# A trunk of float32 feed-forward stages in split products: the order of a pair's matmuls varied from stage to stage

## The chip, the cores and the metric

One core of one Trainium2 chip runs the whole program in one launch. The metric is the device time of that launch in microseconds (us). TensorE (PE) multiplies, and its weight loads stand on a row of their own (PEld); VectorE (DVE) and ScalarE (ACT) do the elementwise work; SyncE (SP) issues the transfers from memory.

## What is computed

Four layers of a decoder trunk on 256 tokens of 1024 features, all in float32. The part that the change touches is the feed-forward stage, of which each layer has two:

```
def swiglu(x, w_gate_up, w_down):              # x [256, 1024], w_gate_up [1024, 2 * 2816], w_down [2816, 1024]
    g, u = jnp.split(x @ w_gate_up, 2, axis=-1)
    return (jax.nn.silu(g) * u) @ w_down

for i in range(4):
    h = h + 0.5 * swiglu(rms_norm(h, norm_ffn1[i]), ffn1_w_gate_up[i], ffn1_w_down[i])
    h = h + mixer[i % 3](rms_norm(h, norm_mix[i]))   # stick-breaking, MoBA or latent attention
    h = h + 0.5 * swiglu(rms_norm(h, norm_ffn2[i]), ffn2_w_gate_up[i], ffn2_w_down[i])
return rms_norm(h, final_norm)
```

## The kernel before

**Split products.** TensorE takes the 4-byte type float32r, which holds fewer bits than float32. So each float32 value is split into a high part and a low part, and a product `w.T @ x` is the sum of high by high, high by low and low by high. The first name is the stationary operand (loaded into the array, 128 x 128), the second the moving one (streamed through, 256 tokens). The moving operand of a feed-forward stage holds a row block's 256 high columns and its 256 low columns side by side. `wide` (L432) therefore makes one product of two matmuls: the high stationary part with 512 moving columns (L434) into a whole bank of PSUM, and the low stationary part with the 256 high columns (L435) into the bank's lower half. `both` (L442, L443) adds the two halves of a bank afterwards. This text calls the first matmul W, the second L, and both together a pair. The mixers use two other forms: `mm3` (L428 to L430) makes three matmuls of 256 columns (stationary parts high, high, low), and `x_proj` (L475 to L477) keeps activations stationary (high, high, low) and streams weights, mostly 512 columns.

**A feed-forward stage.** `ffn` runs `gate_up` for 22 column blocks j of the hidden layer: 8 row blocks k, and for each k one pair for the gate (bank `bs[0]`) and one for the up half (bank `bs[1]`). That is 352 pairs. Two k are issued as one op of the scheduler (one k for the first three j of the program). Then 8 output blocks m each take 22 pairs into one bank, issued in ops of 3, 3, 3 and 2 pairs for each half of the hidden layer: 176 pairs. The stages are numbered here 0 to 7 in the order in which they run, two for each layer with a mixer between them.

**Weights.** A `Chunk` is one transfer into a `raw` buffer (4 of them). ACT copies it into a high part `whi` (L314) and DVE subtracts to get the low part `wlo` (L321), in pieces of up to 1024 columns; there are 6 pairs of such buffers. A piece's buffers come free when the last op that uses it is done.

**Order.** Nothing is ordered by hand. `Program` holds a graph of ops with estimated costs, and `emit` puts them in order by a list schedule: each engine takes the ready op with the lowest due time. One op's instructions stay together. `prep` and `square` (L342 to L345) square each finished row block of h on ACT into one of two `sq` buffers and add it to `acc` on DVE; `norm` then sums over partitions with four short matmuls (L403) and spreads the result with two transposes (L408), which land inside the next stage's products.

Of the kernel before, what the change touches and what calls it, by code (L numbers as in the profile page):

```python
# [28 lines left out]
ZC = SEQ + P  # columns of a head's scores that causality leaves  # L29
# [12 lines left out]
# Gains in one table, 128 rows of a norm to a column.  # L42
# [9 lines left out]
class Slots:  # L52
    """Room for a number of like buffers; some of them are kept from work that can wait."""
# [15 lines left out]
class Buf:  # L69
    """A buffer that the first op of its use takes and the last one gives back."""  # L70
# [7 lines left out]
class Op:  # L78
    """A run of instructions: `ways` has its cost and its emitter for each engine that can do it."""
# [6 lines left out]
class Program:  # L86
    """The program as a graph of short runs of instructions. `emit` puts them in order by a list
    scheduling on estimated costs: each engine's next is the ready one with the least priority
    number, which is the tensor engine's nominal time (us) at the op's place."""
# [32 lines left out]
    def copy(self, cols, fn, deps=(), n=1, **kw):  # L122
        """fn(engine's copy) by whichever of ScalarE and VectorE comes to it first."""
        return self.either({"ACT": (n * 0.095 + 0.00083 * cols, lambda: fn(self.on_act)),
                            "DVE": (n * 0.07 + 0.00104 * cols, lambda: fn(self.on_dve))}, deps, **kw)

    def emit(self):
# [3 lines left out]
        events = []  # time, number, op that becomes ready or buffer that becomes free  # L131
# [58 lines left out]
def fast(n, cols=SEQ):  # L190
    """Time of n float32r products."""
# [4 lines left out]
def trunk_kernel(ctx: ExitStack, tc: tile.TileContext, a: dict, out: bass.AP, nsub: int = 3 * DEPTH):  # L196
# [23 lines left out]
    # ---- room on the chip  # L220
# [5 lines left out]
    parts = Slots([(cp.tile([P, HALF], F32R, name=f"whi{i}"), cp.tile([P, HALF], F32R, name=f"wlo{i}"))  # L226
# [5 lines left out]
    squares = room(2, [SEQ], "sq")  # L232
# [3 lines left out]
    # The normed rows and the activations: a row block's high parts, then its low ones.  # L236
# [8 lines left out]
    # In a mixer the activations' room holds the heads' outputs, then split softplus or latents.  # L245
# [11 lines left out]
    # ---- the tensor engine's clock rises with work: zeros, until the first data come  # L257
# [6 lines left out]
    # ---- constants  # L264
# [8 lines left out]
    # jp[p, i] = i - p  # L273
# [9 lines left out]
    # ---- the weights: DMA, then an exact split of each float32 value into two float32r parts  # L283
    class Chunk:
        """`n` row blocks of `w` columns, `per` of them to a piece. The program's first chunks come
        and are split in smaller runs of row blocks, between `cuts`, the loads in the order `lead`."""

        def __init__(self, ap, n, w, per, cuts=None, lead=20.0):
            self.w, self.per = w, per
# [22 lines left out]
        def hi_fn(self, raw, b, i, k, e):  # L312
            w = self.w
            return lambda: nc.scalar.activation(b.ap[0][:, (k - i) * w:(e - i) * w], raw.ap[:, k * w:e * w], AF.Copy)  # L314

        def lo_fn(self, raw, b, i, k, e):
            w = self.w

            def f():
                s = slice((k - i) * w, (e - i) * w)  # L320
# [3 lines left out]
        def get(self, k):  # L324
            s = slice(k % self.per * self.w, (k % self.per + 1) * self.w)
# [12 lines left out]
    # ---- norms  # L338
    def square(m, dep, lead):
        """Row block m's share of the mean square; gives the op that adds it."""  # L340
# [6 lines left out]
    def prep(m, gain_at, dep, start=False):  # L347
        """Row block m of h is final: its gained, split form for the next products, or its share
        of the result, still to be divided by the rms."""
# [12 lines left out]
    def result(m, dep):  # L362
        """Row block m, gained, transposed into the banks of the result."""
# [14 lines left out]
    def rsqrt(v, scale, keep):  # L378
        """(v * scale + EPS) ** -0.5 of a [128, 2] tile, by Newton's method."""
# [3 lines left out]
        # x is -1/2 of the radicand; the first guess comes from its bits.  # L383
# [657 lines left out]
```

## Time and profile before

| | us |
|---|---|
| median of 3 runs | 1963.67 |
| lowest, highest | 1962.95, 1966.06 |
| span of the profiled execution, first to last instruction | 1960.8 |
| median less that span | 2.9 |

The trace is of one execution. Only its span is recorded, so the 2.9 us around it is the difference from the median. Times in the trace count from the first instruction. A row of the timeline has the start in us, the duration in us, the engine, the line, the operation, the names of the tiles (written<-read), the shapes and a count. The recorded duration of a matmul contains a fixed stretch after its last column, so neighbouring matmuls overlap in the record; the pace is read from start to start.

### The profile page before, as it was taken

Reading aid. Unit: us, or ns where it says so; the run is one execution under the profiler, and the core shown is the slowest. Engines: PE = TensorE matmul, PEld = TensorE weight load, DVE = VectorE, ACT = ScalarE, POOL = GpSimd, SP = SyncE. Lnnn points to the kernel's source line nnn. Section 1 sums busy time; section 2 is a strip of 40 time slices with the busy share of each in tenths; the row PEclk is TensorE's granted clock in tenths of the full one; section 3 lists DMA queues with packets and bytes.
Section 4 is the critical chain, followed back from the end, with each engine's and each line's share of the span. In section 5 each row is a group of like instructions: output and inputs, shape, how many; then the busy total and the mean of one; then the engine's idle time right before and its main releaser. Section 6 shows DMA issues by size and latency. Waiting matters only on the chain.

```text
span 1960.8 us, 30578 instructions
## 1 busy us (share of the span) xinstructions
PE 1946.6 (99%) x11681; PEld 1696.5 (87%) x11681; DVE 1452.3 (74%) x2661; ACT 1144.1 (58%) x2119; POOL 0.4 (0%) x5
## 2 busy tenths in 40 slices
PE   9999999999999999999999999999999999999997
PEld 7888989888888878888888888988888888898886
DVE  8777767777777777877677768877677766668864
ACT  7555556555555555655555557755555555665553
POOL 0000000000000000000000000000000000000000
PEclk9999999999999999999999999999999999999999
DMA  8546435546654653554655454355465456435542
GB/s 301 184 146 220 163 129 175 191 147 204 208 181 147 221 181 109 178 188 147 214 199 191 141 178 155 126 197 178 151 213 197 165 168 220 148 125 198 177 151 81
DMA packets 55875, 342.79 MB, mean 175 GB/s; under 512 B 6192, under 2 KB 7088, under 8 KB 26928
## 3 DMA queue, kind: packets, MB, share of 16 engines
q1 hardware_dynamic: 55728, 340.84, 50.6%
q8 instruction: 92, 1.51, 0.3%
q14 instruction: 55, 0.45, 0.1%
HBM read 339.76 MB, written 1.05 MB: 174 GB/s over the span
## 4 chain that ended last, share of the span: by engine, by line
PE 98%; ACT 1%; DVE 0%; DMA 0%; SPq 0%; issue 0%; DVEq 0%; ACTq 0%
PE ps L434 50%; PE ps L435 26%; PE ps L428 3%; PE ps L429 3%; PE ps L430 3%; PE ps L475 3%; PE ps L476 2%; PE ps L477 2%; PE ps L574 1%; PE ps L624 1%; PE ps L733 1%; PE ps L698 1%; PE ps L771 1%; PE ps L596 1%; PE ps L562 0%; PE ps L576 0%
## 5 line engine op out<-in xcount | busy, mean ns | idle before, releaser
L314 ACT ACTIVATE whi<-raw 128x1024 fp32r<-128x1024 f32 (+2 forms) x738 | 703.0, 954 | 729.7 <-PE ps L434 527.3
L321 DVE TENSOR_TENSOR wlo<-raw,whi 128x1024 fp32r<-128x1024 f32 (+2 forms) x738 | 804.2, 1091 | 396.7 <-ACT whi L314 388.6
L434 PE MATMUL ps<-x,whi 128*128 128x512 f32 x2816 | 998.3, 398 | 1.0 <-DVE acc L345 0.8
L435 PE MATMUL ps<-x,wlo 128*128 128x256 f32 x2816 | 791.8, 281 | 0.2 <-DVE wlo L321 0.2
L434 PEld LDWEIGHTS ps<-x,whi 128*128 128x128 f32 x2816 | 529.7, 188 | 132.2 <-ACT whi L314 2.5
L435 PEld LDWEIGHTS ps<-x,wlo 128*128 128x128 f32 x2816 | 528.8, 188 | 1.3 <-DVE wlo L321 1.2
L434 PE MATMUL ps<-a,whi 128*128 128x512 f32 x1408 | 498.8, 398 | 0.0
L435 PE MATMUL ps<-a,wlo 128*128 128x256 f32 x1408 | 395.7, 281 | 0.0
L434 PEld LDWEIGHTS ps<-a,whi 128*128 128x128 f32 x1408 | 264.8, 188 | 65.1
L435 PEld LDWEIGHTS ps<-a,wlo 128*128 128x128 f32 x1408 | 264.4, 188 | 0.0
L443 DVE TENSOR_TENSOR mid<-ps,mid 128x256 f32<-128x256 f32 x416 | 173.5, 417 | 9.6 <-ACT mid L442 9.6
L442 ACT ACTIVATE mid<-ps 128x256 f32<-128x256 f32 x416 | 151.3, 367 | 11.9 <-PE ps L435 11.9
L515 DVE TENSOR_TENSOR mid<-mid 128x256 f32<-128x256 f32 x176 | 74.6, 424 | 14.2 <-DVE mid L443 0.5
L510 DVE TENSOR_TENSOR mid<-mid,rb 128x256 f32<-128x256 f32 x176 | 74.7, 424 | 6.4 <-ACT rb L411 0.9
L475 PE MATMUL ps<-whi,x 128*128 128x512 f32 (+2 forms) x192 | 74.4, 388 | 0.0
L517 DVE TENSOR_TENSOR a<-mid,a 128x256 fp32r<-128x256 f32 x176 | 73.4, 418 | 1.0 <-ACT a L516 1.0
L428 PE MATMUL ps<-a,whi 128*128 128x256 f32 x256 | 73.9, 289 | 0.0
L428 PE MATMUL ps<-x,whi 128*128 128x256 f32 x256 | 73.0, 285 | 0.0
L476 PE MATMUL ps<-wlo,x 128*128 128x512 f32 (+2 forms) x192 | 72.9, 380 | 0.0
L511 ACT ACTIVATE mid<-mid 128x256 f32<-128x256 f32 x176 | 71.8, 408 | 1.8 <-DVE mid L510 1.7
L477 PE MATMUL ps<-whi,x 128*128 128x512 f32 (+2 forms) x192 | 72.7, 379 | 0.0
L429 PE MATMUL ps<-a,whi 128*128 128x256 f32 x256 | 71.5, 279 | 0.0
(128 smaller groups left out, 1636.7 us busy)
## 6 DMA issues: line engine op xcount, KB each, us to landing
raw<-in_ffn_gu SPq DMA_DIRECT2D x173, 1024.0 KB, 4.8
raw<-in_ffn_dn SPq DMA_DIRECT2D x128, 704.0 KB, 4.1
raw<-in_sb_qk SPq DMA_DIRECT2D x16, 1024.0 KB, 4.9
raw<-in_moba_qkv SPq DMA_DIRECT2D x12, 1024.0 KB, 4.8
raw<-in_sb_v SPq DMA_DIRECT2D x8, 1024.0 KB, 4.7
raw<-in_sb_o SPq DMA_DIRECT2D x8, 1024.0 KB, 4.7
raw<-in_moba_o SPq DMA_DIRECT2D x4, 1024.0 KB, 4.8
raw<-in_mla_o SPq DMA_DIRECT2D x4, 1024.0 KB, 5.0
```

Source lines behind the costliest of these rows:

```text
L314: return lambda: nc.scalar.activation(b.ap[0][:, (k - i) * w:(e - i) * w], raw.ap[:, k * w:e * w], AF.Copy)
L321: nc.vector.tensor_sub(b.ap[1][:, s], raw.ap[:, k * w:e * w], b.ap[0][:, s].bitcast(F32))
L428: nc.tensor.matmul(o, wh, mh, start=first, stop=False, skip_group_check=True)
L429: nc.tensor.matmul(o, wh, ml, start=False, stop=False, skip_group_check=True)
L434: nc.tensor.matmul(o, wh, m2.rearrange("p a b -> p (a b)"), start=first, stop=False, skip_group_check=True)
L435: nc.tensor.matmul(o[:, :SEQ], wl, m2[:, 0, :], start=False, stop=last, skip_group_check=True)
L442: x = g.act(SEQ, lambda: nc.scalar.activation(o(), b.ap[:, SEQ:], AF.Copy), [last], take=take, lead=lead)
L443: return g.dve(SEQ, lambda: nc.vector.tensor_add(o(), b.ap[:, :SEQ], o()), [x], free=[b], lead=lead)
L475: nc.tensor.matmul(o, xs[0][:, k, ts], hi, start=(k == 0), stop=False)
L476: nc.tensor.matmul(o, xs[0][:, k, ts], lo, start=False, stop=False)
L477: nc.tensor.matmul(o, xs[1][:, k, ts], hi, start=False, stop=(k == n - 1))
L510: o = g.dve(SEQ, lambda: nc.vector.tensor_mul(x(), x(), rb[:, 0, :]), [o, rbs[0]])
```

## The change

Every feed-forward stage issues the matmuls of its pairs through a new function `products`, in an order given by two tables, one for gate and up (first and second half of the column blocks j) and one for the down products (first and second half of the output blocks m). The mathematical products are the same in every order. The orders are, for one pair or a group of pairs:

- `each`: W L W L, as before; `each_up`: the same with L added to the bank's upper half; `low_first`: L W L W.
- `three`: the wide matmul is cut in two, high by high into the lower half and high by low into the upper half, each of 256 columns and each with its own load of the same high part, and then L; `three_low_first` has L ahead of them.
- `all`, `all_up`, `all_low_first`, `all_three`: all pairs of the group take the first part, then all the next one (W W L L, for instance). In the gate and up products `pair_all...` groups the two pairs of one k, and plain `all` groups the four pairs of an op; in the down products the group is the op's 3 or 2 pairs.
- `bank`: the op's pairs of one bank together (W W L L), then those of the other.

A number beside an order of gate and up is a shift: the stationary parts are written and read that many float32 elements further on in their buffers. To make room, each `whi` and `wlo` buffer grows by 16 elements, and there is one `sq` buffer in place of two. The estimated costs of the scheduler are the same as before. The diff, without removed comments and texts:

```diff
+ORDERS = [[("each", 0), ("each_up", 0)], [("pair_all", 0), ("pair_all_up", 0)],
+          [("three", 0), ("three_low_first", 0)], [("low_first", 0), ("pair_all_low_first", 0)],
+          [("all", 0), ("bank", 0)], [("each", 16), ("each", 4)],
+          [("pair_all_three", 0), ("three", 16)], [("each", 8), ("each", 0)]]
+DOWN_ORDERS = [["each", "each_up"], ["all", "all_up"], ["three", "three_low_first"], ["low_first", "all_low_first"],
+               ["all_three", "all_three"], ["each", "each"], ["each_up", "all_up"], ["each", "each"]]
...
-    parts = Slots([(cp.tile([P, HALF], F32R, name=f"whi{i}"), cp.tile([P, HALF], F32R, name=f"wlo{i}"))
+    parts = Slots([(cp.tile([P, HALF + 16], F32R, name=f"whi{i}"), cp.tile([P, HALF + 16], F32R, name=f"wlo{i}"))
...
-    squares = room(2, [SEQ], "sq")
+    squares = room(1, [SEQ], "sq")
...
-            w = self.w
-            return lambda: nc.scalar.activation(b.ap[0][:, (k - i) * w:(e - i) * w], raw.ap[:, k * w:e * w], AF.Copy)
+            w, o = self.w, self.shift
+            return lambda: nc.scalar.activation(b.ap[0][:, o + (k - i) * w:o + (e - i) * w], raw.ap[:, k * w:e * w], AF.Copy)
...
-                s = slice((k - i) * w, (e - i) * w)
+                s = slice(self.shift + (k - i) * w, self.shift + (e - i) * w)
...
-            s = slice(k % self.per * self.w, (k % self.per + 1) * self.w)
+            s = slice(self.shift + k % self.per * self.w, self.shift + (k % self.per + 1) * self.w)
...
+    def products(order, items, k0, k1):
+        started, left = set(), {}
+
+        def put(item, part, cols):
+            o, hi, lo, m2, k = item
+            key = id(o)
+            first = k == k0 and key not in started
+            started.add(key)
+            left[key] -= 1
+            last = k == k1 and left[key] == 0
+            w, m, at = ((hi, m2.rearrange("p a b -> p (a b)"), slice(0, 2 * SEQ)),
+                        (lo, m2[:, 0, :], slice(0, SEQ)),
+                        (lo, m2[:, 0, :], slice(SEQ, 2 * SEQ)),
+                        (hi, m2[:, 0, :], slice(0, SEQ)),
+                        (hi, m2[:, 1, :], slice(SEQ, 2 * SEQ)))[part]
+            nc.tensor.matmul(o[:, at], w, m, start=first, stop=last, skip_group_check=True)
+
+        WIDE, LOW, LOW_UP, HH, HL = range(5)
+        kinds = {"each": [WIDE, LOW], "each_up": [WIDE, LOW_UP], "low_first": [LOW, WIDE],
+                 "three": [HH, HL, LOW], "three_low_first": [LOW, HH, HL],
+                 "all": [WIDE, LOW], "all_up": [WIDE, LOW_UP], "all_low_first": [LOW, WIDE],
+                 "all_three": [HH, HL, LOW], "bank": [WIDE, LOW]}
+        parts_ = kinds[order]
+        for it in items:
+            left[id(it[0])] = left.get(id(it[0]), 0) + len(parts_)
+        if order.startswith("all"):
+            for part in parts_:
+                for it in items:
+                    put(it, part, None)
+        elif order == "bank":
+            for key in dict.fromkeys(id(it[0]) for it in items):
+                for part in parts_:
+                    for it in items:
+                        if id(it[0]) == key:
+                            put(it, part, None)
+        else:
+            for it in items:
+                for part in parts_:
+                    put(it, part, None)
...
-                            wide(bs[p].ap, hi[:, w], lo[:, w], x2[:, k], k == 0, k == NT - 1)
+                            items.append((bs[p].ap, hi[:, w], lo[:, w], x2[:, k], k))
+                    if order in ("each", "each_up", "low_first", "three", "three_low_first"):
+                        for i in range(0, len(items), 2):
+                            products(order, items[i:i + 2], 0, NT - 1)
+                    elif order.startswith("pair_"):
+                        for i in range(0, len(items), 2):
+                            products(order[5:], items[i:i + 2], 0, NT - 1)
+                    else:
+                        products(order, items, 0, NT - 1)
...
-            evac(j, *gate_up(j, cuts, lead, 1 if first else 2))
+            order, shift = ORDERS[2 * l + which][j >= NF // 2]
+            evac(j, *gate_up(j, cuts, lead, 1 if first else 2, order, 0 if first else shift))
...
+            order = DOWN_ORDERS[2 * l + which][m >= NT // 2]
...
-                        for f in fs:
-                            j = half * FH + f
-                            wide(b.ap, *c.get(f), a2[:, j], j == 0, j == NF - 1)
+                        items = [(b.ap, *c.get(f), a2[:, half * FH + f], half * FH + f) for f in fs]
+                        if order.startswith("all") or order == "bank":
+                            products(order, items, 0, NF - 1)
+                        else:
+                            for it in items:
+                                products(order, [it], 0, NF - 1)
```

## Rows read from the trace of the kernel before

**Rows 1.** The page: its first line, the busy time of each engine (us, share of the span, instructions), and the chain of work that ended last by engine.

```profile
span 1960.8 us, 30578 instructions
...
PE 1946.6 (99%) x11681; PEld 1696.5 (87%) x11681; DVE 1452.3 (74%) x2661; ACT 1144.1 (58%) x2119; POOL 0.4 (0%) x5
...
PE 98%; ACT 1%; DVE 0%; DMA 0%; SPq 0%; issue 0%; DVEq 0%; ACTq 0%
```

**Rows 2.** The waits, longest first: who waited for whom, us in total, times, longest. First the longest of all engines, then two of the longest of PE.

```profile
ACT whi L314 <- PE ps L434: 527.3, 482, 3.2
...
PE ps L372 <- ACT nat L373: 2.3, 1, 2.3
...
PE ps L434 <- DVE acc L345: 0.8, 1, 0.8
```

**Rows 3.** The down products of stage 0: the count of W matmuls (ns min/median/max, first and last start), and from PE's timeline the first W, the last W and the mixer's first matmul behind its L.

```profile
L434 PE MATMUL ps<-a,whi x176: 397/398/398, 132.6 to 194.4; 128*128 128x512 f32 x176
...
132.57 0.40 PE L434 MATMUL ps<-a,whi 128*128 128x512 f32 x1
...
194.41 0.40 PE L434 MATMUL ps<-a,whi 128*128 128x512 f32 x1
...
194.76 0.28 PE L428 MATMUL ps<-x,whi 128*128 128x256 f32 x1
```

**Rows 4.** PE's groups by line and shape over the whole span: count, busy us, mean ns of one, idle before.

```profile
L434 PE MATMUL ps<-x,whi 128*128 128x512 f32 x2816 | 998.3, 398 | 1.0 <-DVE acc L345 0.8
L435 PE MATMUL ps<-x,wlo 128*128 128x256 f32 x2816 | 791.8, 281 | 0.2 <-DVE wlo L321 0.2
...
L429 PE MATMUL ps<-x,whi 128*128 128x256 f32 x256 | 71.4, 279 | 0.0
...
L476 PE MATMUL ps<-wlo,x 128*128 128x512 f32 x160 | 62.8, 392 | 0.0
```

**Rows 5.** `mm3` in the output projection after the first mixer: the count of its first matmul, and from the timeline the first and the last of them.

```profile
L428 PE MATMUL ps<-a,whi x41: 281/281/282, 295.9 to 310.1; 128*128 128x256 f32 x41
...
295.93 0.28 PE L428 MATMUL ps<-a,whi 128*128 128x256 f32 x1
...
310.07 0.28 PE L428 MATMUL ps<-a,whi 128*128 128x256 f32 x1
```

**Rows 6.** `mm3` in the output projection after the second mixer: the same rows, then the W of two pairs in a row, among the first of stage 3, right behind it.

```profile
L428 PE MATMUL ps<-a,whi x30: 276/276/277, 789.4 to 799.2; 128*128 128x256 f32 x30
...
789.38 0.28 PE L428 MATMUL ps<-a,whi 128*128 128x256 f32 x1
...
799.24 0.28 PE L428 MATMUL ps<-a,whi 128*128 128x256 f32 x1
...
799.92 0.40 PE L434 MATMUL ps<-x,whi 128*128 128x512 f32 x1
...
800.27 0.40 PE L434 MATMUL ps<-x,whi 128*128 128x512 f32 x1
```

**Rows 7.** `x_proj` with 512 moving columns: in the second mixer the count of L475 with first and last start; then the start of that mixer, where such matmuls follow a feed-forward pair.

```profile
L475 PE MATMUL ps<-whi,x x19: 392/392/392, 745.5 to 757.8; 128*128 128x512 f32 x19
...
745.48 0.39 PE L475 MATMUL ps<-whi,x 128*128 128x512 f32 x1
...
757.84 0.39 PE L475 MATMUL ps<-whi,x 128*128 128x512 f32 x1
...
684.74 0.28 PE L435 MATMUL ps<-a,wlo 128*128 128x256 f32 x1
684.86 0.39 PE L475 MATMUL ps<-whi,x 128*128 128x512 f32 x1
685.09 0.39 PE L476 MATMUL ps<-wlo,x 128*128 128x512 f32 x1
685.32 0.40 PE L477 MATMUL ps<-whi,x 128*128 128x512 f32 x1
```

**Rows 8.** PE's timeline around a norm's short matmuls: inside `mm3` of the first mixer, and inside the products of stage 1, where the first row follows the two transposes L408.

```profile
201.83 0.50 PE L403 MATMUL ps<-onesf,acc 128*128 128x1 f32 x4
202.19 0.36 PE L428 MATMUL ps<-x,whi 128*128 128x256 f32 x1
202.40 0.28 PE L429 MATMUL ps<-x,whi 128*128 128x256 f32 x1
...
322.30 0.48 PE L434 MATMUL ps<-x,whi 128*128 128x512 f32 x1
322.62 0.28 PE L435 MATMUL ps<-x,wlo 128*128 128x256 f32 x1
```

**Rows 9.** The timeline inside gate and up of stage 0: an L matmul, and the load of the next W.

```profile
100.30 0.28 PE L435 MATMUL ps<-x,wlo 128*128 128x256 f32 x1
100.31 0.19 PEld L434 LDWEIGHTS ps<-x,whi 128*128 128x128 f32 x1
```

**Rows 10.** The `sq` buffers at the end of the first mixer: the last square on ACT, the last two adds on DVE, and DVE's first instruction on the norm's sums.

```profile
312.58 0.40 ACT L344 ACTIVATE sq<-gh 128x256 f32<-128x256 f32 x1
...
313.43 0.41 DVE L345 TENSOR_TENSOR acc<-acc,sq 128x256 f32<-128x256 f32 x1
314.90 0.42 DVE L345 TENSOR_TENSOR acc<-acc,sq 128x256 f32<-128x256 f32 x1
318.39 0.15 DVE L384 TENSOR_SCALAR nx<-ps 128x2 f32<-128x2 f32 x1
```

More of the change, by code (lines that the diff above doesn't have):

```diff
@@ L284, in trunk_kernel, with __init__ @@
     class Chunk:
-        def __init__(self, ap, n, w, per, cuts=None, lead=20.0):
-            self.w, self.per = w, per
+        def __init__(self, ap, n, w, per, cuts=None, lead=20.0, shift=0):
+            self.w, self.per, self.shift = w, per, shift
             self.pieces = []
@@ L487, in ffn, with gate_up @@
         xdeps = list(state["x"])
-        def gate_up(j, cuts, lead, step):
-            c = Chunk(gu[l, j], NT, 2 * P, NT // 2, cuts, lead)
+        def gate_up(j, cuts, lead, step, order, shift):
+            c = Chunk(gu[l, j], NT, 2 * P, NT // 2, cuts, lead, shift)
             bs = [bank(2), bank(2)]
@@ L494, in f @@
                 def f(ks=ks):
+                    items = []
                     for k in ks:
```

## The prediction

> **What bounds the kernel now.** I read the page first, then the waits, then PE's timeline, then the pace of each kind of matmul. The page says PE: busy 1946.6 of 1960.8 us, and 98% of the chain that ended last [rows 1]. The waits say that nobody holds PE up: its longest wait is 2.3 us, at the very end, while ACT waited 527.3 us in all for PE to give weight buffers back [rows 2]. So the splitting of the weights runs ahead and is throttled by PE. What counts is only the pace at which PE takes matmuls, and the reader should see that this pace is not one number.
>
> Paces, each from a first and a last start:
> - Pair in a feed-forward stage: (194.41 - 132.57) / 175 = 353.4 ns [rows 3].
> - `mm3`, three matmuls of 256 columns: slow stretches at (310.07 - 295.93) / 40 = 353.5 ns, or 117.8 each [rows 5], and fast ones at (799.24 - 789.38) / 29 = 340.0 ns, or 113.3 each [rows 6]. It is the same code with another mixer in front.
> - `x_proj`, 512 columns behind 512 columns: (757.84 - 745.48) / 54 = 228.9 ns [rows 7].
>
> The recorded duration follows the pace with a constant of 163 ns on top: 281 - 117.8, 276 - 113.3, 392 - 228.9 [rows 5, 6, 7]. The pair can therefore be divided: L has 281, so 118 ns, and W has 398, so 235 ns [rows 4], together 353. So a 512-column matmul takes 6.5 ns less (353.4 - 118 = 235.4 against 228.9) where its neighbours are 512 wide too than where it alternates with 256. The drop is there at once when a run of W begins behind a feed-forward pair: 684.86, 685.09, 685.32 [rows 7].
>
> The page's mean of 279 for L429 lies three fifths of the way from 276 to 281 [rows 4, 5, 6]: the mixers' 256-column matmuls are slow about 3 times in 5.
>
> **The change part by part.** The columns streamed are the same in every order; only neighbours, loads and addresses change.
>
> *Grouped orders (`all`, `pair_all`, `bank` and their variants).* They put W behind W. Counting W matmuls whose predecessor is a W:
> - stage 1, gate and up: 22 x 8 = 176; down: groups of 3, 3, 3, 2 give 7 for each half of the hidden layer, 14 for each m, 112 for 8 m
> - stage 3, second half of gate and up: 88; of down: 56
> - stage 4, `all` over four pairs: 11 x 4 x 3 = 132; `bank`: 11 x 8 = 88
> - stage 6, second half of down: 56
>
> That is 708. At 6.5 ns each they give 4.6 us. Between 0 (if the 235 belongs to the feed-forward's operands and not to the neighbours) and 6.5 I take 6.5, because the step comes within one matmul of the switch [rows 7]. As many L stand behind an L. They cost 117.8 or 113.3, against 118 now: 0 to 3.3 us; I take 0, the slow pace that follows feed-forward work.
>
> *`three` and its variants.* Stage 2 whole (352 + 176), stage 4 down (176), stage 6 gate and up (352): 1056 products of three 256-column matmuls, with 1056 more matmuls and loads. This is the pattern of `mm3` itself, whose three loads are also covered. The slow pace gives 353.5 against 353.4, so nothing; the fast one 13.4 less, 14.1 us over all. Which one holds depends on the way in. `mm3` begins at the slow pace directly behind feed-forward pairs, 194.76 on, and after a norm's short matmuls it goes on (202.19 to 202.40, 0.21 with a load not covered) [rows 8]. The long fast stretch of rows 6 stands behind the small matmuls of an attention head, and it ends with the first pairs (800.27 - 799.92 = 0.35) [rows 6]. The `three` stretches are entered from feed-forward work, so I take slow: 0.
>
> *`each_up` and `low_first`.* The cycle of sizes is the same, and a bank's columns are written again after no fewer columns than in `mm3`, which puts three matmuls on the same 256: 0, at both paces seen.
>
> *Shifts.* 352 pairs have stationary parts at 4 or 8 elements, 176 pairs and 176 of the `three` products at 16. No row of the kernel has a load at such an offset. From below it is nothing. From above it is a load that its neighbour does not cover: the first W behind a norm takes 322.62 - 322.30 = 0.32 us instead of 0.235, so 85 ns [rows 8]. For all 1584 loads of these stretches that is 135 us. I take 0: loads are 16 elements at most away from where they were, and the work that hides them is unchanged. The thin cover is the L of 118 ns: the next W's load starts with it [rows 9]. The Trainium skill, "SBUF — State Buffer", Specifications (TRN2), gives lines of 16 bytes; the shifts are 16, 32 and 64 bytes, so by it no load touches a further line and the term is 0 as well, which no row here tests. ACT's and DVE's writes at the shifted places are hidden: ACT waits for PE's buffers [rows 2].
>
> *One `sq` buffer.* A square must wait for the add before it. At a mixer's end the last square ran at 312.58, ahead of the add that began at 313.43, so it would come about 1.3 us later (313.43 + 0.41 - 312.58), and with it the add at 314.90. The norm's sums are used by DVE at 318.39 only [rows 10]: 3 us of cover. Without that cover, 8 norms x 1.3 us = 10 us; I take 0. In ACT's order a late square holds back weight copies behind it, which have the six buffers' lead.
>
> Sum: -4.6 us on a span of 1960.8, so 1956.2; with the 2.9 us that the median stands above this span, 1959.
>
> **The rivals.** A measurement of this kernel tells 0.2% (3.9 us) from nothing.
>
> *Order does not matter.* If W costs 235 because of its own operands, every term is 0 and the time stays at 1963.7. For it: the pace is the same in gate and up, which alternates banks, as in down, which does not. Against it: rows 7. The Trainium skill, "TensorE: Matmul & The Clock Gate", Back-to-back issue gap, has such a rule: columns / 2.4 + 2.5 ns per matmul, whatever the neighbour. By it a pair would take 325 ns and the 1056 extra matmuls would cost 2.6 us, 1966.3. The trace's 353.4 does not agree.
>
> *The fast pace.* If the `three` stretches, or most of them, run like rows 6, 14.1 us more go: 1959.1 - 14.1 = 1945. If half of them do, 1952. For it: two fifths of the mixers' 256-column matmuls are fast. Against it: the way in.
>
> *Shifted loads are slow* (slower than before). If the W's load at 4 or 8 elements no longer fits under the L, each of 352 pairs loses up to 85 ns: 1959 + 30 = 1989. It decides from 24 ns a pair, (4.6 + 3.9) us / 352. For it: the L is the shortest cover there is, and no load here is unaligned. Against it: in fast `mm3` three loads fit into 340 ns, so a load needs under 114 and has a little room.
>
> **How the numbers follow.** Grouping saves and `three` is neutral: 0.42, 1956 to 1962 by itself, around 1959. Nothing changes: 0.25, 1961 to 1966. Fast pace in part or whole: 0.18, 1945 to 1956. Shifts or something like them cost: 0.15, 1967 to 2000. The likeliest gives 1959. The range from 1946 to 1969 leaves out the far ends of the last two cases. Faster by over 0.2% means under 1959.7: about six tenths of the first case and all of the third, 0.45. Slower means over 1967.6: 0.17, the fourth case and a little of the second. Within: 0.38.
>
> **What the profile after would show.** Stage 1's 176 down pairs, now 62.2 us, would take 0.7 us less (112 x 6.5), and the W would show 392 and 398 side by side. Stage 2 would keep its length to 0.2 us at a mean of 281 for its 256-column matmuls; 276 there would mean the fast pace. Stages 0, 5 and 7 would keep theirs; a longer W in the halves of stages 5 and 7 with shifts 4 and 8 would show slow loads. PE's waits would stay under 5 us. I am wrong if W behind W keeps 398, if the 256-column matmuls lock to 276, or if a shifted stretch stands out.

## The result, and the profile after

The changed kernel takes 1952.89 us (median of 3 runs, 1950.61 to 1953.46) against 1963.67: 0.994 of the time, with an interval of 0.9921 to 0.996. The profiled span fell by 12.0 us, from 1960.8 to 1948.8. The time lies in the range and on the side that I gave most chance, but 6 us under the forecast, and the experiments show that most of the reasons were wrong, so the hit is luck: a part that I had costed at nothing is worth more than the whole change, and the orders, which are worth something alone, give part of it back.

The page of the changed kernel (busy time and share of the span by engine, then the chain that ended last):

```profile
span 1948.8 us, 32589 instructions
PE 1934.1 (99%) x12737; PEld 1744.7 (90%) x12737; DVE 1451.0 (74%) x2661; ACT 1147.5 (59%) x2119; POOL 0.4 (0%) x5
...
PE 98%; ACT 1%; DMA 0%; DVE 0%; SPq 0%; issue 0%; DVEq 0%; ACTq 0%
```

As in [rows 1], PE is the chain. Its longest waits (count, total and longest in us) stay as short as those of [rows 2], so all that was gained or lost is the pace of its matmuls:

```profile
PE ps L380 <- ACT nat L381: 2.3, 1, 2.3
...
PE ps L462 <- ACT whi L322: 1.4, 1, 1.4
```

The groups of one shape on PE (count, busy us, mean ns of one, idle before). Against 398 and 281 of [rows 4], the W now has a mean of 394 and the L 280; the 256-column `x,whi` of L462 are the halves of a cut W:

```profile
L462 PE MATMUL ps<-x,whi 128*128 128x512 f32 x2112 | 698.3, 394 | 1.5 <-ACT whi L322 1.4
L462 PE MATMUL ps<-x,wlo 128*128 128x256 f32 x2816 | 696.0, 280 | 0.2 <-DVE wlo L329 0.2
L462 PE MATMUL ps<-a,whi 128*128 128x512 f32 x1056 | 337.7, 394 | 0.0
...
L437 PE MATMUL ps<-x,whi 128*128 128x256 f32 x256 | 72.0, 281 | 0.0
```

Means hide where it went. I took the pace of a pair (768 columns in any order) from first to last start in every half-stage, without the stretches around a norm's short matmuls, the waits at the start of the program and the transposes of the result at its end. Before, it was 353.3 ns in all of them. "First" and "second" are the halves of gate and up. The last two columns belong to two experiments told below: the change's orders without its buffers, and its buffers without its orders.

| stage | orders: first, second, down as it ran | after, ns a pair | orders alone | buffers alone |
|---|---|---|---|---|
| 0 | each, each_up, each_up | 346.2, 345.8, 346.8 | 353.3 | 345.2 to 347.4, all stages |
| 1 | pair_all, pair_all_up, all_up | 350.0, 350.0, 351.0 | 346.9, 346.7, 348.2 | |
| 2 | three, three_low_first, three_low_first | 354.1, 354.1, 353.9 | 351.8, 353.3, 353.3 | |
| 3 | low_first, pair_all_low_first, all_low_first | 344.5, 349.6, 350.9 | 353.1, 346.8, 348.3 | |
| 4 | all, bank, all_three | 349.2, 350.0, 352.3 | 346.9, 346.7, 340.0 | |
| 5 | each at 16, each at 4, each | 347.0, 351.5, 346.2 | 353.3 | |
| 6 | pair_all_three, three at 16, all_up | 350.8, 350.6, 351.0 | 353.3, 353.3, 348.1 | |
| 7 | each at 8, each, each | 349.6, 345.8, 346.7 | 353.3 | |

Each entry stands for 176 pairs. Summed over the column "after", (353.3 - pace) x 176 gives 16.1 us, which is also what the feed-forward stretches lost in the traces (1501.5 to 1485.4). The mixers got 4.2 longer (443.0 to 447.2). The two together make 11.9 of the 12.0 us.

The stages where the change alters least gained most. Stage 0 keeps its order in the first half and only writes another half of the bank in the second, and its pairs fell from 353.3 to 346. In the timeline of PE (start, duration), the first two rows below are the first and last W of that second half: (129.76 - 69.23) / 175 = 345.9 ns, against 353.4 in [rows 3].

```profile
69.23 0.40 PE L462 MATMUL ps<-x,whi 128*128 128x512 f32 x1
...
129.76 0.39 PE L462 MATMUL ps<-x,whi 128*128 128x512 f32 x1
...
1819.88 0.39 PE L462 MATMUL ps<-x,whi 128*128 128x512 f32 x1
...
1822.33 0.39 PE L462 MATMUL ps<-x,whi 128*128 128x512 f32 x1
...
1822.67 0.39 PE L462 MATMUL ps<-x,whi 128*128 128x512 f32 x1
...
1825.06 0.40 PE L462 MATMUL ps<-x,whi 128*128 128x512 f32 x1
```

The four later rows, of stage 7 with plain `each`, show what 346 is made of. Seven pairs take 2.45 us (350 each), the next seven 2.39 (341.4): the pace changes from one piece of weights to the next, that is from one pair of buffers to the next. By the program's allocation, in the kernel before all six `whi` and `wlo` buffers begin at 128 bytes past a multiple of 256. With 16 elements (64 bytes) more in each they begin alternately at (high, low) = (128, 192) and (0, 64). The moving operands, `x2` and `a2`, stay at 64 in both kernels, modulo 256.

**A correction to the reading of the code.** In the down loop of the changed kernel the function handed to the scheduler binds `fs`, `half`, `c` and `b`, but not `order`:

```
order = DOWN_ORDERS[2 * l + which][m >= NT // 2]
...
    def f(fs=fs, half=half, c=c, b=b):
```

It runs when all is emitted, after the loop is done, so all down products of a stage take the second entry of the table. Stage 3's table begins with `low_first`, yet from its first block on the trace shows three L and then three W:

```profile
920.31 0.52 PE L462 MATMUL ps<-a,wlo 128*128 128x256 f32 x3
920.67 0.85 PE L462 MATMUL ps<-a,whi 128*128 128x512 f32 x3
921.36 0.52 PE L462 MATMUL ps<-a,wlo 128*128 128x256 f32 x3
```

So there are 820 W behind a W (708 + 56 in stage 3 + 56 in stage 6), not 708, and "first and second half of the output blocks" in the section on the change is what the table says, not what runs.

### The profile page after: what moved, and what is told of

The parts are those of the page before. It is cut to its first block, busy times and chain, and to the rows that moved or that the text cites. A ratio compares the mean times of both kernels' runs of the same rounds, so it can differ in the third digit from the quotient of the medians.

```text
span 1948.8 us, 32589 instructions
## 1 busy us (share of the span) xinstructions
PE 1934.1 (99%) x12737; PEld 1744.7 (90%) x12737; DVE 1451.0 (74%) x2661; ACT 1147.5 (59%) x2119; POOL 0.4 (0%) x5
## 4 chain that ended last, share of the span: by engine, by line
PE 98%; ACT 1%; DMA 0%; DVE 0%; SPq 0%; issue 0%; DVEq 0%; ACTq 0%
PE ps L462 76%; PE ps L436 3%; PE ps L437 3%; PE ps L438 3%; PE ps L525 3%; PE ps L527 2%; PE ps L526 2%; PE ps L638 1%; PE ps L688 1%; PE ps L797 1%; PE ps L762 1%; PE ps L835 1%; PE ps L660 1%; PE ps L626 0%; PE ps L640 0%; PE ps L760 0%
## 5 line engine op out<-in xcount | busy, mean ns | idle before, releaser
L462 PE MATMUL ps<-x,whi 128*128 128x512 f32 (+1 forms) x3520 | 940.5, 348 | 1.5 <-ACT whi L322 1.4
L462 PE MATMUL ps<-x,wlo 128*128 128x256 f32 x2816 | 696.0, 280 | 0.2 <-DVE wlo L329 0.2
L462 PEld LDWEIGHTS ps<-x,whi 128*128 128x128 f32 x3520 | 579.5, 188 | 57.8 <-ACT whi L322 2.7
L462 PEld LDWEIGHTS ps<-x,wlo 128*128 128x128 f32 x2816 | 517.7, 188 | 35.2 <-DVE wlo L329 0.7
L462 PE MATMUL ps<-a,whi 128*128 128x512 f32 (+1 forms) x1760 | 451.6, 348 | 0.0
L462 PE MATMUL ps<-a,wlo 128*128 128x256 f32 x1408 | 321.7, 280 | 0.0
L462 PEld LDWEIGHTS ps<-a,whi 128*128 128x128 f32 x1760 | 285.5, 188 | 27.7
L462 PEld LDWEIGHTS ps<-a,wlo 128*128 128x128 f32 x1408 | 246.9, 188 | 17.3
L436 PE MATMUL ps<-a,whi 128*128 128x256 f32 x256 | 74.2, 290 | 0.0
L436 PE MATMUL ps<-x,whi 128*128 128x256 f32 x256 | 73.5, 287 | 0.0
L437 PE MATMUL ps<-x,whi 128*128 128x256 f32 x256 | 72.0, 281 | 0.0
```

The lines of the kernel that those rows point to most:

```text
L436: nc.tensor.matmul(o, wh, mh, start=first, stop=False, skip_group_check=True)
L437: nc.tensor.matmul(o, wh, ml, start=False, stop=False, skip_group_check=True)
L462: nc.tensor.matmul(o[:, at], w, m, start=first, stop=last, skip_group_check=True)
```

## The experiments

All are changed forms of these two kernels, timed beside the kernel before. In the expectations, theory A in its forms is that the pace depends on where the operands lie; what else a letter stands for is said in the text itself. Only one time was taken where "one run" stands.

**The buffers without the orders** (the changed kernel):

```diff
-ORDERS = [[("each", 0), ("each_up", 0)], [("pair_all", 0), ("pair_all_up", 0)],
...
+ORDERS = [[('each', 0), ('each', 0)], [('each', 0), ('each', 0)], ...
+DOWN_ORDERS = [['each', 'each'], ['each', 'each'], ...
```

> The changed kernel with every order put back to each and every shift to 0: only the 16 more elements per weight buffer and the single sq buffer are left. Theory A (the buffers' places set the pace): every feed-forward pair takes 346 ns, as in stages 0 and 7 of the changed kernel (345.8), against 353.3 before: 4224 pairs x 7.3 ns = 31 us less in those stages, some 4 us more in the mixers as the changed kernel shows, about 1937 us. Rival B (the orders made the gain, and stages 0, 5 and 7 got faster for another reason that follows the neighbouring stages): little or no gain, 1958 to 1964 us.

1937.68 us, ratio 0.9863 (0.9847 to 0.9879). The order is that of the kernel before, instruction for instruction in a pair; the buffers are 64 bytes longer and there is one `sq`. The feed-forward stretches take 1473.3 us, 28.2 less than before, the mixers 447.1, 4.1 more. In the profiled execution the start of the program is some 2.6 us longer, in part by the wait in the first row below (0.8 in [rows 2]); the paces alone save 30.9 us, 7.3 ns a pair, as expected. In the last stage, second half of gate and up, the timeline's first and last W give (1862.41 - 1801.88) / 175 = 345.9 ns.

```profile
PE ps L458 <- DVE acc L349: 2.2, 1, 2.2
```
```profile
1801.88 0.40 PE L458 MATMUL ps<-x,whi 128*128 128x512 f32 x1
...
1862.41 0.39 PE L458 MATMUL ps<-x,whi 128*128 128x512 f32 x1
```

So the room made for the shifts is worth 27 us, and the orders together with the shifts cost 15 of them, by the medians as by the paces (30.9 against 16.1).

**The orders without the buffers.** All orders of the change, no shift, old buffers, two `sq`:

```diff
-    parts = Slots([(cp.tile([P, HALF + 16], F32R, name=f"whi{i}"), ...
+    parts = Slots([(cp.tile([P, HALF], F32R, name=f"whi{i}"), ...
...
-    squares = room(1, [SEQ], "sq")
+    squares = room(2, [SEQ], "sq")
```

> The orders of the change without its buffers: no pad, no shift, two sq buffers as before. Theory A: stages with each keep 353.3 ns a pair; grouping may save what the prediction gave it, 6.5 ns for each of 708 W behind a W, 4.6 us, about 1959 us; three stays at 353.5. Rival B: the whole gain of the change, about 1953 us.

1952.93 us, ratio 0.9941 (0.9926 to 0.9956): the first figure of the expectation was missed by 6 us. The time is the one of rival B, but this is not the gain of the changed kernel: stages 0, 5 and 7 stay at 353.3 here and gain there, and stages 1 and 4 gain more here than there. By the table, the grouped orders save 8.4 us and `all_three` 2.3; `three`, `low_first` and `each_up` save next to nothing. Stage 1, `pair_all`, PE's timeline (two W, then two L, and so on), then the groups of that stretch, then the first two of these W each by itself and stage 4's `all_three` (count, shortest/median/longest ns, first and last start):

```profile
374.65 0.62 PE L458 MATMUL ps<-x,whi 128*128 128x512 f32 x2
375.11 0.40 PE L458 MATMUL ps<-x,wlo 128*128 128x256 f32 x2
375.35 0.62 PE L458 MATMUL ps<-x,whi 128*128 128x512 f32 x2
375.81 0.39 PE L458 MATMUL ps<-x,wlo 128*128 128x256 f32 x2
376.04 0.62 PE L458 MATMUL ps<-x,whi 128*128 128x512 f32 x2
```
```profile
L458 PE MATMUL ps<-x,whi 128*128 128x512 f32 x175 | 54.7, 393 | 0.0
L458 PE MATMUL ps<-x,wlo 128*128 128x256 f32 x174 | 34.3, 278 | 0.0
```
```profile
L458 PE MATMUL ps<-x,whi x1: 388/388/388, 374.7 to 374.7; 128*128 128x512 f32 x1
L458 PE MATMUL ps<-x,whi x1: 398/398/398, 374.9 to 374.9; 128*128 128x512 f32 x1
```
```profile
L458 PE MATMUL ps<-a,whi x350: 276/276/276, 1106.7 to 1165.9; 128*128 128x256 f32 x175
L458 PE MATMUL ps<-a,wlo x174: 276/276/276, 1107.3 to 1165.7; 128*128 128x256 f32 x174
```

Averaged over the stretch, from each start to the next, a cycle of W W L L takes 226 + 236 + 118 + 113.5 = 693.5 ns, against 706.6 for two pairs before. It is the W behind an L that got shorter, 388 recorded, while all 88 W behind a W in this stretch keep 398. Nor does a longer group save more: `all` puts three W of four behind a W, `pair_all` and `bank` one of two, and all three end at 346.7 to 346.9 a pair. Alone, buffers give 0.9863 and orders 0.9941; together they give 0.994. The two effects do not add. At the new places grouped orders run 3 to 5 ns a pair slower than `each` in all eight entries of the table, and the `three` of stage 2 8 ns slower.

**A table of places.** One kernel, `each` throughout, in which every half-stage of gate and up has its own start of the high and low parts, and each half of the down products one start for both (the first three j of the program keep the start without a shift). Room was made by 128 more elements in each buffer and one less `nat` and `turned`. A second kernel has 48 in the place of the 0 in the diff's last line, which moves `x2` and `a2` from 64 to 0 modulo 256:

```diff
-        def __init__(self, ap, n, w, per, cuts=None, lead=20.0, shift=0):
+        def __init__(self, ap, n, w, per, cuts=None, lead=20.0, shift=(0, 0)):
...
-    gh = cp.tile([P, G_ALL + NT * SEQ], F32, name="gh")
+    gh = cp.tile([P, G_ALL + NT * SEQ + 0], F32, name="gh")
```

The moving operands at 64:

> Every order is each. The weight buffers are 512 bytes longer, so that all high and low parts can start at any place modulo 512 bytes, and the activations x2 and a2 stay at 64 modulo 256 as in the kernel before. The 16 half-stages of gate and up take the starts of (high, low) modulo 256 at all combinations of 0, 64, 128, 192; those of down take equal starts from 0 to 384 in other steps. One turned, one nat and one sq buffer are given up for room. Theory A1 (what counts is the place of the stationary part alone, by lines of the memory that it crosses): paces between 340 and 353 by the starts' own residues, the same whatever the activations' place. Theory A2 (what counts is the distance between stationary and moving operand): paces between 340 and 353 by the residue of start minus 64. Rival B: all half-stages at one pace.

The moving operands at 0:

> The same table of starts, with the activations x2 and a2 at 0 modulo 256 bytes. Theory A1: every half-stage has the pace that it has with the activations at 64. Theory A2: the table is that of the other run moved on by 64 bytes. A third possibility, that the moving operand's own start counts: all half-stages shift together, down to some 325 ns a pair if aligned reads cost nothing beyond the columns.

1948.78 and 1957.92 us (one run each), with these paces of a pair in ns; starts in bytes modulo 256, before the slash with the moving operands at 64, behind it with them at 0:

| high \ low | 0 | 64 | 128 | 192 |
|---|---|---|---|---|
| 0 | 353.3 / 352.6 | 350.0 / 346.7 | 347.1 / 346.8 | 346.7 / 350.0 |
| 64 | 346.7 / 351.7 | 353.4 / 353.2 | 347.2 / 350.0 | 346.7 / 353.2 |
| 128 | 352.9 / 351.9 | 340.1 / 353.3 | 353.3 / 351.1 | 350.0 / 346.7 |
| 192 | 346.7 / 348.7 | 352.0 / 353.3 | 347.7 / 346.7 | 351.1 / 353.3 |

The range is 340.1 to 353.4, 13 ns in the same order of the same matmuls. For (128, 64): (1102.80 - 1043.28) / 175 = 340.1 ns in the first kernel. Below are the first and last W of its timeline, then the groups of one shape of that half-stage, then those of the second kernel at the same starts, with 394 and 285 for 389 and 276:

```profile
1043.28 0.40 PE L459 MATMUL ps<-x,whi 128*128 128x512 f32 x1
...
1102.80 0.39 PE L459 MATMUL ps<-x,whi 128*128 128x512 f32 x1
```
```profile
L459 PE MATMUL ps<-x,whi 128*128 128x512 f32 x176 | 59.9, 389 | 0.0
L459 PE MATMUL ps<-x,wlo 128*128 128x256 f32 x176 | 48.7, 276 | 0.0
```
```profile
L459 PE MATMUL ps<-x,whi 128*128 128x512 f32 x174 | 61.5, 394 | 0.0
L459 PE MATMUL ps<-x,wlo 128*128 128x256 f32 x173 | 49.4, 285 | 0.0
```

Is it the absolute place or the distance to the moving operand? Moving everything by 64 bytes should leave the pace if the distance counts. 31 settings of the first kernel have one at the same distance modulo 256 in the second (16 in gate and up, 15 in down): 23 of them agree within 1 ns (11 and 12). Of the 32 with the same absolute starts, which also stand in the same half-stage, 8 agree, and a quarter is what any two entries of the table do. So the distance counts, but it is not all: the best setting has 340.1 in the first kernel and 351.7 at the same distance in the second. In steps of 16 bytes (down products, equal starts) the pace also jumps: 353.2 at 0, 349.9 at 16, 346.8 at 32, 353.2 at 48, 346.7 at 96. In the run told next the first three repeat within 1 ns, and the last two are 346.6 and 353.3.

**The same table in reverse order** over the half-stages, to see whether a setting or its place in the program makes the pace:

```diff
-ORDERS = [[('each', 96, 96), ('each', 96, 112)], ... [('each', 16, 0), ('each', 16, 16)]]
+ORDERS = [[('each', 16, 16), ('each', 16, 0)], ... [('each', 96, 112), ('each', 96, 96)]]
```

> The scan with the activations at 64 again, its table of starts run from the last entry to the first, so that each combination stands in another stage and behind another neighbour. If the place decides: each combination keeps its pace within 1 ns, (128, 64) at 340. If history decides: the paces stay with the stages and not with the starts.

1952.1 us (one run). 13 of the 16 settings repeat within 0.6 ns, and 13 of the 16 down ones within 1 ns. Three of gate and up don't: (0, 64) 348.5 against 350.0, (192, 128) 353.3 against 347.7, and the best one, (128, 64), 351.6 against 340.1, as its groups show beside those above. So the places decide most of the paces, and what ran before them some:

```profile
L459 PE MATMUL ps<-x,whi 128*128 128x512 f32 x163 | 57.7, 396 | 0.0
L459 PE MATMUL ps<-x,wlo 128*128 128x256 f32 x164 | 46.0, 280 | 0.0
```

**The best place everywhere.** High parts at 128, low at 64, all stages `each`, one `sq`, buffers of the old size with fillers between:

```diff
+    his = [cp.tile([P, HALF], F32R, name=f"whi{i}") for i in range(6)]
+    cp.tile([P, 240], F32, name="gap")
+    los = [cp.tile([P, HALF], F32R, name=f"wlo{i}") for i in range(6)]
+    cp.tile([P, 16], F32, name="back")
```

> Every order is each, no shift, buffers of the old size; all high parts lie at 128, all low parts at 64 and the activations at 64 modulo 256 bytes, by two unused tiles and one sq buffer less. This is the one combination that ran at 340.1 ns a pair in the scan with the activations at 64. If the places set the pace: 340 ns in all 4224 pairs, 13.3 x 4224 = 56 us less than before in the feed-forward stages, the mixers within 5 us of before: about 1908 us (1903 to 1913). If the 340 of the scan was an accident of what ran just before it: some half-stages at 346 to 353, 1915 to 1960 us.

1938.59 us, ratio 0.9868 (0.9852 to 0.9884), 30 us over the first figure of the expectation and within its second case. The setting has three paces: 340.0 in stages 2, 3 and 5, 350.0 in 0, 1 and 7, 353.3 in 4 and 6. A pace holds for over 100 us, through gate and up and down alike, and changes inside a stage only where short matmuls stand: a norm's column sums and transposes, and in stage 7 the transposes of the result. The timeline at one of them, then groups of one shape in two windows:

```profile
505.54 0.39 PE L461 MATMUL ps<-x,whi 128*128 128x512 f32 x1
...
506.24 0.39 PE L461 MATMUL ps<-x,whi 128*128 128x512 f32 x1
...
506.59 0.38 PE L415 MATMUL ps<-identf,ny 128*128 128x128 f32 x2
...
508.17 0.39 PE L461 MATMUL ps<-x,whi 128*128 128x512 f32 x1
...
509.19 0.39 PE L461 MATMUL ps<-x,whi 128*128 128x512 f32 x1
```
```profile
L461 PE MATMUL ps<-x,whi 128*128 128x512 f32 x286 | 97.3, 389 | 0.0
L461 PE MATMUL ps<-x,wlo 128*128 128x256 f32 x286 | 78.9, 276 | 0.0
...
L461 PE MATMUL ps<-x,whi 128*128 128x512 f32 x166 | 58.7, 396 | 0.0
```

Two pairs ahead of the transposes (L415) take 0.70 us, three behind them 1.02 (340 each). The means of 389 and 276 are of 520 to 676 us; the 396 is of 1040 to 1160, stage 4, with the same places and order.

Two things follow from the same run. What a norm sets does not look like a new draw in each execution: stages 1 and 7, which have the same mixer in front, go through the same paces, and so do stages 4 and 6, and the four times lie within 3.9 us, where 340.0 in place of 353.3 in one stage is 7 us. And it is not the writes of ACT and DVE to the moved buffers that set the pace: in the down products of stage 2 (622.5 to 676 us, the W, then the busy time of each engine) both work part of the time, and no W leaves 389; the W of [rows 3] stay at 397 to 398 in the same way.

```profile
L461 PE MATMUL ps<-a,whi x158: 389/389/389, 622.4 to 675.8; 128*128 128x512 f32 x158
...
622.50:676.00 53.50, 53.50 (x316) 47.32 (x315) 39.60 (x64) 31.94 (x52) 0.00 (x0) 1.00 0.63 220
```

The columns of the second row are the length, then PE, PEld, DVE, ACT and POOL, the granted clock, the share of the DMA engines and GB/s.

**These places with the change's orders:**

```diff
-ORDERS = [[('each', 0), ('each', 0)], [('each', 0), ('each', 0)], ...
+ORDERS = [[('each', 0), ('each_up', 0)], [('pair_all', 0), ('pair_all_up', 0)], ...
```

> The same places with the ten orders of the change (no shifts). If the places alone set the pace, 340 ns a pair whatever the order, about 1908 us. If order and places act together, as the orders without pads suggest (346.7 grouped against 353.3 each), some orders lose the good pace: stages 1 to 4 and 6 at 343 to 353, 1915 to 1940 us.

1960.33 us (one run): `pair_all` and `bank` take 356 to 357 ns a pair, `all` 348.5, `three` 353.3, grouped down products 350.9, `all_three` 355, and `each` 353.3 in stage 0, 340.0 in stage 5 and 350.0 in stage 7. At the places where `each` had its best pace, two of the grouped orders have the worst of all runs. Place and order act together.

**One `sq` alone** (the kernel before with `squares = room(1, [SEQ], "sq")`):

> The kernel before with one sq buffer in place of two, nothing else. It moves the activations by 1024 bytes, which leaves all places the same modulo 1024. Expected: no change, 1961 to 1966 us. If the distance over more than 1024 bytes counts, the feed-forward pace leaves 353.3.

1964.37 against 1963.65 us, ratio 1.0 (0.9991 to 1.0009), and all pairs at 353.3.

**Two places that alternate.** As in the table, but the two pieces of a transfer have a start each:

```diff
-            w, o = self.w, self.shift[0]
+            w, o = self.w, self.shift[i // self.per][0]
```

> Order each everywhere, activations at 64 modulo 256 bytes. In gate and up the two pieces of a chunk now start at different places, as the pads of the change made them: first the 16 half-stages with (high, low) of (128, 64) or (0, 64) in one piece and another place in the other piece; in down 16 places in steps of 16 and 32 bytes, the same for both pieces. If a change of place from piece to piece sets the state anew, as the piece at (0, 64) of the changed kernel suggests (341.4 ns behind a piece at (128, 192), 350 by itself in the scan): half-stages with a mean of 341 to 345. If only a norm's short matmuls set it: means that are those of the single places, 346 to 351.

1936.01 us (one run). (128, 64) with (0, 64) held 340.0 in the one half-stage that had it in that order, and the down products behind it kept 340.0 at two other places; it had 344.0 in the reverse order. The other combinations of gate and up had 343 to 352.

**That alternation everywhere:** high parts alternately at 128 and 0, low ones at 64, by fillers of 96, 144 and 16 elements, no longer buffers and no shift:

```diff
+    his = {i: cp.tile([P, HALF], F32R, name=f"whi{i}") for i in (0, 2, 4)}
+    cp.tile([P, 96], F32, name="gap")
+    his |= {i: cp.tile([P, HALF], F32R, name=f"whi{i}") for i in (1, 3, 5)}
```

> Order each, buffers of the old size, low parts and activations at 64 modulo 256 bytes, and high parts alternately at 128 and at 0, so that every piece of weights differs from the one before it. In the scan of two places this pair gave 340.0 ns in the half-stage that no norm interrupts, and 344.0 in the one with the start of the program in it. If a change of place sets the state anew every 2.8 us: 340 to 342 ns in nearly all half-stages, also behind a norm's short matmuls, 13 x 4224 = 55 us less in the feed-forward stages, about 1908 us (1903 to 1918). If the state is still drawn by the norms: half-stages at 346 to 353 among them, 1920 to 1945 us.

1928.49 us (median of 5 runs, 1924.21 to 1930.7), ratio 0.9811 (0.9798 to 0.9824): better than the kernel before by 1.9% and, by the two ratios, than the changed one by 1.3%. It is 20 us over the first figure of the expectation and within its second case: the alternation does not bring every stage to 340. Stages 1, 4, 6 and 7 run at 340 ns; gate and up of stages 0, 2, 3 and 5 at 350 to 351.7, and then 340 from the down products on. Groups of stage 1 (375 to 490 us), then of stage 2's gate and up (557 to 614):

```profile
L463 PE MATMUL ps<-a,whi 128*128 128x512 f32 x175 | 59.5, 389 | 0.0
L463 PE MATMUL ps<-x,whi 128*128 128x512 f32 x164 | 55.8, 389 | 0.0
...
L463 PE MATMUL ps<-x,whi 128*128 128x512 f32 x163 | 57.4, 395 | 0.0
L463 PE MATMUL ps<-x,wlo 128*128 128x256 f32 x163 | 45.7, 281 | 0.0
```

## Why the prediction was right in its total and wrong in its steps

- **The missing term.** The prediction prices what the shifts do, but not the 16 elements that each buffer grows by. That pad moves the starts in all six pairs of buffers, modulo 256, even where the shift is 0. "Loads are 16 elements at most away from where they were, and the work that hides them is unchanged" took the length of the move for the only question. "Stages 0, 5 and 7 would keep theirs" is where it fails: stage 0 fell from 353.3 to 346. Measured alone, the pad is -27 us. This is also the term that I could have asked the trace of before about: `mm3` ran at 340.0 and at 353.5 with the same code [rows 5, 6], and I put that down to the way in alone.
- **Grouped orders**, predicted -4.6. At the old places they give -8.4. The direction was right and the division wrong: I gave W 229 behind a W and 235 behind an L. It is 236 behind a W and 226 behind the Ls, and the L behind an L, costed at 118, takes 113.5. My own sign of being wrong, W behind W that keeps 398, is there. The saving is 6.6 ns a pair, twice what one W in two pairs would give. At the changed places it turns: `each` takes 346 there and grouped orders 349 to 351. I had borrowed the step from `x_proj` [rows 7], whose operands lie elsewhere; no run tried whether that is why it does not carry over.
- **`three`**, predicted 0 at the slow pace. Right at the old places (353.3 in stage 6, 351.8 to 353.3 in stage 2), apart from `all_three`, where the rival of the fast pace came true for 176 pairs (2.3 us). At the new places 354 in stage 2, which is 8 ns above `each` there. The means of 281 that I named as the sign are in the trace after, as the first two rows below show (groups of one shape, 557 to 619 us; the last two are of 1326 to 1387 us, stage 5), and still `three` is not neutral against the 346 that `each` gets:

```profile
L462 PE MATMUL ps<-x,whi 128*128 128x256 f32 x351 | 62.2, 281 | 0.0
L462 PE MATMUL ps<-x,wlo 128*128 128x256 f32 x177 | 49.6, 281 | 0.0
...
L462 PE MATMUL ps<-x,whi 128*128 128x512 f32 x175 | 61.6, 395 | 0.0
L462 PE MATMUL ps<-x,wlo 128*128 128x256 f32 x174 | 48.9, 281 | 0.0
```

- **Shifts**, predicted 0. Against 345.8 for `each` without a shift, 16 elements cost 1.2 ns a pair, 8 cost 3.8 and 4 cost 5.7: 1.9 us for the three half-stages. Each was run in one half-stage only, and one setting can have several paces, so the sizes are of this run. `three` at 16 is 3.5 ns a pair faster than `three` at 0, 0.6 us back. The last two rows above are the shift of 4: the W has a mean of 395 there and the L 281, against 394 and 280 in the whole run, so the half does not stand out as the sign would have it. The rival had the direction right; the price is under its 24 ns. The Trainium skill, "SBUF — State Buffer", Specifications (TRN2), gives lines of 16 bytes. I had worked out from it that these shifts cost nothing, and the trace doesn't agree: 16 bytes make 5.7 ns. No run took a whole load out, so whether it is the load that suffers is open.
- **`low_first` and `each_up`**, predicted 0: 353.1 and 353.3 at the old places, right. At the new ones `low_first` gives 344.5, the best of the changed kernel.
- **One `sq`**, predicted 0: right, ratio 1.0.
- **Order doesn't matter** as a rival: wrong by 8.4 us and more. The rule weighed there comes from the Trainium skill, "TensorE: Matmul & The Clock Gate", Back-to-back issue gap, which states it for the isolated gap of a matmul and not for a stream with weight loads. The 325 ns a pair worked out from it were never seen; the least in any run is 340.0.
- **The mixers**, not in the sum: +4.2 us. It comes with the buffers (+4.1 with the pad alone, +0.2 with the orders alone). I did not take it apart further; a hint is that `mm3`'s second matmul, now L437, has a mean of 281, where [rows 4] had 279: the slow pace of [rows 5] throughout.

The total came out near because, by the paces in the traces, -31 of the pad, +15 of orders and shifts at the new places and +4 of the mixers sum to -12, where I had -4.6. The pad and the mixers were not in my sum, and the orders and shifts had the other sign there, so a total in the range is luck.

**What stays open.** The runs show that the pace depends on the places of the operands, mostly through the distance between stationary and moving starts, on the order, and on something that persists. What collides is not shown. The Trainium skill, "TensorE: Matmul & The Clock Gate", Step-by-step: what each phase is for, says that TensorE reads the moving operand and the weights through two independent ports, so that loading the next weights takes nothing from the running matmul. By that alone a distance between the two should not matter; the table of places shows 13 ns. Nor is it shown what decides the pace behind a norm: the same places and order gave 340.0, 350.0 and 353.3.

## What to carry to other kernels

When orders of matmuls are compared, keep the addresses of their operands fixed, or vary them on purpose: a pad, a shift or a filler of a few dozen bytes is a variable of its own, here larger than any order, and the two do not add. A table of starts over the half-stages of one run shows the spread cheaply, but a good setting must be run everywhere before it is believed, since one setting can have several paces. And in a deferred emitter, look which loop variables are bound: what a table says is not always what runs.

## What the runs showed of the hardware that I had not expected

- With TensorE's granted clock at 0.997 to 0.998 over every run told here, the level of 2.4 GHz, a stream of pairs of 512 and 256 columns takes mostly 340.0, 346.7, 350.0 or 353.3 ns a pair, steps of some 3.3 ns, without any wait in the profile.
- The pace follows the byte distance between the stationary parts and the moving operand (23 of 31 settings within 1 ns, 8 of 32 by absolute starts), in steps as small as 16 bytes: 353.2, 349.9 and 346.8 at 0, 16 and 32.
- A pace can hold for over 100 us and be set anew by a few short matmuls: 350 ahead of two transposes, 340 behind them, with the same places and order.
- In the order W W L L at the old places it is the W behind the Ls that gets short (388 recorded), while the W behind a W keeps the 398 of W L W L.
- High parts alternately at two places, with the low parts at a third, take 1.9% off the kernel before, more than any order tried.
